# A decoder layer on one core: order and place of small operations in the head, earlier partial projections, and a new end of the expert stage

## The chip, the core and the metric

The kernel runs on one core of a Trainium2 chip. TensorE (PE) multiplies matrices, its weight loads are shown apart (PEld); VectorE (DVE), ScalarE (ACT) and GpSimd (POOL) work on tiles, SyncE (SP) starts almost all transfers. Each engine works off its own queue in order. The metric is the device time of one execution in microseconds.

## What is computed

The reference is one decoder layer on 256 tokens of 2048 columns. Cut to what matters here:

```python
mod = silu(c) @ w_ada + b_ada                   # 6 x 2048: shifts, scales, gates
sh_a, sc_a, gt_a, sh_m, sc_m, gt_m = split(mod, 6)
h = rmsnorm(x, norm_mix_g) * (1 + sc_a) + sh_a
x = x + gt_a * hybrid_mixer(h, ...)             # h @ w_in, MLA attention, mLSTM, gates, w_out
h = rmsnorm(x, norm_ffn_g) * (1 + sc_m) + sh_m
x = x + gt_m * hier_moe(h, ...)                 # router: 1 of 4 groups, 2 of its 8 experts
```

The router picks two of 32 experts for each token. The transfers of one execution move 561 MB, most of it weights.

## The kernel before

**Layout.** Activations lie transposed, 128 columns of the model on the partitions and 256 tokens along a tile, so that a row block k (of KT = 16) is 128 rows of the weights. `big` has 9 buffers of 1 MB (`u8`) for raw weights and a few large tiles, `w4` 3 of the same size (`w8`) for weights split in two, PSUM 8 banks. SyncE's queue follows the program's order (`manual_schedule`); on the other engines a scheduler orders instructions by its own estimate, except where `keep_in_program_order` pins them.

**Start.** cond = silu(c) spread over 128 partitions; the squares of x summed over partitions by 16 matmuls with a matrix of ones (ssum, L208); rstd by Ln and Exp (L157, L158).

**Head, 21 to 182 us.** A loop over k. Each row block loads three tiles on SyncE: ada tile 16 + k and ada tile k (1 MB each), and the 11 column blocks of w_in that are needed first (w_head, 704 KB). VectorE multiplies an ada tile with cond and sums along the row (L143): a column of mod. From the first comes gs = (mod + 1 + b) * gain (L151), from the second mod + b (L146). Then hp = x * gs * rstd (L805) on VectorE, h = hp + mod (L808) on ScalarE, hh = h rounded to fp32r (L811), hl = h - hh (L812). For k < WHOLE = 8 TensorE multiplies in fp32 as it is, 11 matmuls (22 passes) into six banks `hb` (L810). From k = 8 the weights are split into a rounded part and a rest (`split`, L186 on ScalarE and L187 on VectorE, tile `whl`), and three matmuls (`mm3`: L199, L200, L201) take the place of one. `push` splits a tile at once and emits its matmuls when the next has been pushed.

From k = 8 the loop also works on other columns of w_in: `first_halves` gives 14 pieces, six pairs of q/k columns of the mLSTM, v and o, each over row blocks 0 to 7 alone. `half_pair` loads 1 MB of `w_half`, runs 96 passes into a bank `hp`, and `keep_part` copies the bank to a tile `part` (L322, ScalarE). After the loop the second halves run over row blocks 8 to 15, and `add_part` adds them (L328, VectorE).

**Middle, to 780 us.** Attention, mLSTM, gates, w_out and the router; TensorE works nearly all the time.

**Experts, to the end.** Experts are ranked by their number of tokens, and stacks of four ranks (HEAVY, LIGHT) are worked off, the slabs read through a ring of buffers (`fetch_used`; a slab of an unused expert is not read). In `stack`, each of four chunks of w_down multiplies into a bank `yb`, f = 0 to 3 over the rows of four slabs; `finish` splits it into yh (L1314, ScalarE) and yl (L1315, VectorE); `combine` multiplies by the tokens' weights (L1324, L1325, banks `ob`) and `accumulate` adds to xs (L1231). A chunk is combined after the next one's matmuls, the last at the end. `store` writes 4 of 16 row blocks out.

Then follow two parts for rare cases: a last stack under `tc.If` (L1403), if its first rank has tokens, and a loop over experts with too many tokens (L1409, count read at L1408). In the execution shown both are jumped over.

## Time and profile before

| | us |
|---|---|
| median of three executions (1630.15 to 1633.23) | 1631.26 |
| the profiled execution | 1634.16 |
| its span, first to last instruction | 1632.3 |
| TensorE busy | 1360.1 (83%) |
| VectorE busy | 816.4 (50%) |
| ScalarE busy | 504.9 (31%) |
| mean granted TensorE clock | 0.933 |

The profiled execution lies 2.90 us above the median; 1.86 us of it lie outside the span. The chain of work that ended last is TensorE's by 51% and transfers' by 34%. A stage table (busy time of each engine in stretches of the span) is the best first view, since the stages have different limits: the head, the middle and the experts each look unlike the mean.

### The profile page before, as it was taken

Reading aid. Unit: us, or ns where it says so; the run is one execution under the profiler, and the core shown is the slowest. Engines: PE = TensorE matmul, PEld = TensorE weight load, DVE = VectorE, ACT = ScalarE, POOL = GpSimd, SP = SyncE. Lnnn points to the kernel's source line nnn. Section 1 sums busy time; section 2 is a strip of 40 time slices with the busy share of each in tenths; the row PEclk is TensorE's granted clock in tenths of the full one; section 3 lists DMA queues with packets and bytes.
Section 4 is the critical chain, followed back from the end, with each engine's and each line's share of the span. In section 5 each row is a group of like instructions: output and inputs, shape, how many; then the busy total and the mean of one; then the engine's idle time right before and its main releaser. Section 6 shows DMA issues by size and latency. Waiting matters only on the chain.

```text
span 1632.3 us, 24652 instructions
## 1 busy us (share of the span) xinstructions
PE 1360.1 (83%) x9726; PEld 1004.2 (62%) x9726; DVE 816.4 (50%) x1177; ACT 504.9 (31%) x720; POOL 90.5 (6%) x91
## 2 busy tenths in 40 slices
PE   7799998999999999999796696978668857567665
PEld 5598997899999989989662354645323313213212
DVE  5878699879766789986411431343111301201202
ACT  3134765446645574444311110321100101001000
POOL 0150013000000010121000000000000000000000
PEclk9999999999999999999997799999889987867998
DMA  9988767878676779874589999999999999999995
GB/s 381 369 307 328 272 230 283 317 287 303 243 273 235 276 271 413 322 292 151 228 362 382 371 392 420 374 422 396 411 420 421 420 422 421 421 421 421 421 421 223
DMA packets 78462, 560.96 MB, mean 344 GB/s; under 512 B 8705, under 2 KB 8961, under 8 KB 11905
## 3 DMA queue, kind: packets, MB, share of 16 engines
q1 hardware_dynamic: 78050, 558.84, 86.6%
q8 instruction: 80, 1.31, 0.3%
q10 hardware_dynamic: 288, 0.45, 0.1%
q14 instruction: 44, 0.36, 0.1%
HBM read 569.74 MB, written 2.10 MB: 350 GB/s over the span
## 4 chain that ended last, share of the span: by engine, by line
PE 51%; DMA 34%; DVE 9%; ACT 3%; issue 2%; POOL 0%; SPq 0%; DVEq 0%; POOLq 0%; ACTq 0%
DMA ring<-in_w_gu_dram 22%; DMA ring<-in_w_dn_dram 11%; PE gu L1285 6%; PE ga L199 4%; PE ga L201 4%; PE ga L200 4%; DVE raw L143 4%; PE yb L1285 3%; DVE whl L187 2%; PE hp L201 2%; PE hp L199 2%; PE hp L200 2%; PE xb L1259 2%; PE wo L199 1%; PE wo L201 1%
## 5 line engine op out<-in xcount | busy, mean ns | idle before, releaser
L1285 PE MATMUL gu<-ring,xg 128*32 128x512 f32 (+1 forms) x1664 | 256.5, 714 | 131.2 <-DMA ring<-in_w_gu_dram 131.0
L187 DVE TENSOR_TENSOR whl<-raw,whl 128x1024 fp32r<-128x1024 f32 (+1 forms) x222 | 267.7, 1213 | 95.5 <-ACT whl L186 95.0
L186 ACT ACTIVATE whl<-raw 128x1024 fp32r<-128x1024 f32 (+1 forms) x222 | 229.6, 1038 | 266.7 <-PE ga L201 62.7
L1285 PEld LDWEIGHTS gu<-ring,xg 128*32 128x32 f32 (+1 forms) x1664 | 63.6, 130 | 304.3 <-DMA ring<-in_w_gu_dram 157.5
L143 DVE SCALAR_TENSOR_TENSOR raw<-raw,cond 128x2048 f32<-128x2048 f32 x96 | 220.4, 2297 | 15.2 <-DMA raw<-in_w_ada_dram 15.2
L1285 PE MATMUL yb<-ring,aT 128*32 128x512 f32 (+1 forms) x832 | 130.4, 723 | 76.7 <-DMA ring<-in_w_dn_dram 75.3
L199 PE MATMUL ga<-hh,whl 128*128 128x256 f32 x512 | 149.6, 292 | 0.0
L201 PE MATMUL ga<-hh,whl 128*128 128x256 f32 x512 | 145.0, 283 | 1.4 <-DVE whl L187 1.3
L200 PE MATMUL ga<-hl,whl 128*128 128x256 f32 x512 | 144.8, 283 | 0.0
L1285 PEld LDWEIGHTS yb<-ring,aT 128*32 128x32 f32 (+1 forms) x832 | 33.7, 131 | 156.9 <-issue 115.9
L1251 DVE TENSOR_REDUCE wc<-cb 128x1 f32<-128x256 f32 x7 | 3.0, 425 | 208.7 <-PE cb L1248 208.7
L1231 DVE SCALAR_TENSOR_TENSOR xs<-ob,mod,xs 128x256 f32<-128x256 f32 x112 | 46.4, 476 | 119.0 <-PE ob L1325 119.0
L187 DVE TENSOR_TENSOR whl<-rawb,whl 128x1024 fp32r<-128x1024 f32 x36 | 43.0, 1222 | 116.5 <-ACT whl L186 116.4
L199 PEld LDWEIGHTS ga<-hh,whl 128*128 128x128 f32 x512 | 97.9, 191 | 5.1 <-issue 3.5
L201 PEld LDWEIGHTS ga<-hh,whl 128*128 128x128 f32 x512 | 97.9, 191 | 2.0 <-DVE whl L187 2.0
L200 PEld LDWEIGHTS ga<-hl,whl 128*128 128x128 f32 x512 | 98.0, 191 | 1.0 <-issue 0.7
L201 PE MATMUL hp<-hh,whl 128*128 128x256 f32 x320 | 91.0, 284 | 3.4 <-DVE whl L187 3.3
L199 PE MATMUL hp<-hh,whl 128*128 128x256 f32 x320 | 92.0, 287 | 0.0
L200 PE MATMUL hp<-hl,whl 128*128 128x256 f32 x320 | 90.5, 283 | 0.0
L1303 ACT ACTIVATE s<-gu 128x512 f32<-128x512 f32 x7 | 4.2, 597 | 273.9 <-PE gu L1285 273.9
L186 ACT ACTIVATE whl<-rawb 128x1024 fp32r<-128x1024 f32 x36 | 36.8, 1053 | 163.1 <-DMA rawb<-in_w_dn_dram 76.2
L201 PE MATMUL gu<-xgh,whl 128*128 128x258 f32 x256 | 72.1, 285 | 2.2 <-DVE whl L187 2.2
(418 smaller groups left out, 2846.0 us busy)
## 6 DMA issues: line engine op xcount, KB each, us to landing
ring<-in_w_gu_dram SPq DMA_DIRECT2D x208, 1024.0 KB, 14.6
ring<-in_w_dn_dram SPq DMA_DIRECT2D x104, 1024.0 KB, 15.5
raw<-in_w_ada_dram SPq DMA_DIRECT2D x96, 1024.0 KB, 6.9
raw<-in_w_blk_dram SPq DMA_DIRECT2D x32, 1024.0 KB, 5.1
raw<-in_w_half_dram SPq DMA_DIRECT2D x20, 1024.0 KB, 6.8
raw<-in_w_out_dram SPq DMA_DIRECT2D x16, 1024.0 KB, 6.6
raw<-in_w_head_dram SPq DMA_DIRECT2D x16, 704.0 KB, 6.6
rawb<-in_w_gu_dram SPq DMA_DIRECT2D x10, 1024.0 KB, 8.9
```

What stands on the lines that cost most here:

```text
L143: vec.scalar_tensor_tensor(raw, raw, 1.0, cond, op0=ALU.mult, op1=ALU.mult, accum_out=mod[:, i:i + 1])
L186: keep(act.activation(hi, raw, AF.Copy))
L187: keep(vec.tensor_tensor(lo, raw, hi.bitcast(F32), op=ALU.subtract))
L199: pe.matmul(out, wh, xh, start=first, stop=False)
L200: pe.matmul(out, wh, xl, start=False, stop=False)
L201: pe.matmul(out, wl, xh, start=False, stop=last)
L1231: vec.scalar_tensor_tensor(xs[:, d], src, mod[:, 80 + d:81 + d], xs[:, d], op0=ALU.mult, op1=ALU.add)
L1251: vec.tensor_reduce(wc, cb[:, :T], axis=AX.X, op=ALU.add)
L1259: pe.matmul(b[:, i * P:(i + 1) * P], xr[tt][:, k * P:(k + 1) * P], gt[tt], start=tt == 0, stop=tt == 1)
L1285: return lambda: pe.matmul(out[j * C:(j + 1) * C, :], x[:, k * P + j * C:k * P + (j + 1) * C], ws[j][:, cut], start=first, stop=stop)
L1303: act.activation(s, gu[0], AF.Silu)
```

## The change

- *Start:* the squares are added up on VectorE in part; 6 matmuls instead of 16.
- *Row blocks:* gs and mod + b are each one ScalarE operation on a column (with gbias = (1 + b) * gain worked out once). VectorE's order is pinned: product for tile 16 + k, hl of the block before, product for tile k, hp. For k >= 8 hl is a plain subtraction from an h that ScalarE writes.
- *Quarters:* the first half of each of the six q/k pairs is cut in two. Row blocks 0 to 3 of it (`quarter`, 512 KB, 24 passes after the split of half a tile) run after blocks 4 to 7 (1, 2, 1, 2 pieces); row blocks 4 to 7 stay in `first_halves`, now with `add_part` instead of `keep_part`. The weights' layout in memory is changed to match.
- *Loads:* const goes from block 0 to block 10, the router's weights from ScalarE's queue to SyncE's.
- *Experts:* in the last stack's last chunk the four slabs are read in two parts each (f = 0 to 2, then f = 3); chunk 2 is combined ahead of f = 3; `finish` works in two halves.
- *Rare cases:* the router works out one number (`spill[33]`) that is not zero if either case occurs, and one `tc.If` holds both.

```diff
@@ -136,22 +136,21 @@
     vec.tensor_scalar(bada1, col("b_ada", 0, 96), 1.0, None, op0=ALU.add)
+    gbias = keep.tile([P, KT], F32, name="gbias")
+    vec.tensor_tensor(gbias, bada1[:, KT:2 * KT], col("mix_g", 0, KT), op=ALU.mult)
@@ -200,12 +199,19 @@
         pe.matmul(out, wh, xl, start=False, stop=False)
         pe.matmul(out, wl, xh, start=False, stop=last)
 
-    ssum = bank("ssum")
+    ssum, sums = bank("ssum"), [None, None]
     for i in range(8):
-        sq = pair("sq")
-        act.activation(sq, xs[:, 2 * i:2 * i + 2], AF.Square)
+        sq = t2("sq")
+        act.activation(by2(sq), xs[:, 2 * i:2 * i + 2], AF.Square)
+        if sums[i // 6] is None:
+            sums[i // 6] = sq
+        elif i < 6:
+            vec.tensor_tensor(sums[0], sums[0], sq, op=ALU.add)
+        if i == 7:
+            sums.append(sq)
+    for i, sq in enumerate(sums):
         for j in range(2):
-            pe.matmul(ssum[:, :T], ones, sq[:, j], start=i + j == 0, stop=i + j == 8)
+            pe.matmul(ssum[:, :T], ones, sq[:, j * T:(j + 1) * T], start=i + j == 0, stop=i + j == 3)
     rstd = t2("rstd")
     rsqrt(rstd[:, :T], ssum[:, :T], D)
 
@@ -289,12 +295,22 @@
-    def half_pair(src, half, after):
-        raw = load(src[half])
+    def half_pair(src, half, after, quarters=(0, 1)):
+        q0, q1 = quarters[0], quarters[-1] + 1
+        raw = u8("raw")[:, :(q1 - q0) * 1024]
+        nc.sync.dma_start(raw, src[half][:, q0 * 1024:q1 * 1024])
         b = bank("hp")
-        for i in range(2):
-            push_block(raw[:, i * 1024:(i + 1) * 1024], b[:, i * T:(i + 1) * T], 8, lambda k: hhk(k + 8 * half),
-                       lambda k: hlk(k + 8 * half), (lambda: after(b)) if i else None)
+        for q in quarters:
+            def fn(wh, wl, q=q):
+                for i in range(2):
+                    for j in range(4):
+                        k, s = 8 * half + 4 * q + j, slice((4 * i + j) * P, (4 * i + j + 1) * P)
+                        mm3(b[:, i * T:(i + 1) * T], wh[:, s], wl[:, s], hhk(k), hlk(k), q == q0 and i + j == 0,
+                            q == q1 - 1 and i == 1 and j == 3)
+            push(raw[:, (q - q0) * 1024:(q - q0 + 1) * 1024], fn, (lambda: after(b)) if q == q1 - 1 else None)
+
+    def quarter(i):
+        half_pair(w_half[i], 0, keep_part(("qk", i)), (0,))
@@ -332,7 +348,7 @@
 
     def first_halves():
         for i in range(6):
-            half_pair(w_half[i], 0, keep_part(("qk", i)))
+            half_pair(w_half[i], 0, add_part(("qk", i)), (1,))
             yield
         for nh in range(2):
             yield from v_half(nh, 0, keep_part(("v", nh, 0), ("v", nh, 1)))
@@ -787,34 +803,47 @@
+    def lower(k, h):
+        tc.keep_in_program_order(vec.tensor_tensor(hlk(k), h, hhk(k).bitcast(F32), op=ALU.subtract))
...
+    above = None
     for k in range(KT):
-        ada(16 + k)
-        ada(k)
+        tc.keep_in_program_order(ada(16 + k))
+        if above:
+            lower(*above)
+        tc.keep_in_program_order(ada(k))
         raw = u8("raw")[:, :HEAD_N * P]
         nc.sync.dma_start(raw, w_head[k])
-        if k == 0:
+        if k == 10:
...
-        ada_gain(0, k, k + 1, 16, "mix_g")
-        ada_bias(k, k + 1)
+        act.activation(gs[:, 0, k:k + 1], mod[:, 16 + k:17 + k], AF.Identity, bias=gbias[:, k:k + 1], scale=col("mix_g", k))
+        act.activation(mod[:, k:k + 1], mod[:, k:k + 1], AF.Identity, bias=col("b_ada", k))
         hp = t2("hp")
-        vec.scalar_tensor_tensor(hp[:, :T], xs[:, k], gs[:, 0, k:k + 1], rstd[:, :T], op0=ALU.mult, op1=ALU.mult)
+        h = hp[:, T:]
+        tc.keep_in_program_order(vec.scalar_tensor_tensor(hp[:, :T], xs[:, k], gs[:, 0, k:k + 1], rstd[:, :T],
+                                                          op0=ALU.mult, op1=ALU.mult))
+        act.activation(h, hp[:, :T], AF.Identity, bias=mod[:, k:k + 1])
+        act.activation(hhk(k), h, AF.Copy)
+        above = (k, h)
...
         if k < WHOLE:
-            h = hp[:, T:]
-            act.activation(h, hp[:, :T], AF.Identity, bias=mod[:, k:k + 1])
...
-            act.activation(hhk(k), h, AF.Copy)
-            vec.tensor_tensor(hlk(k), h, hhk(k).bitcast(F32), op=ALU.subtract)
...
+            while k > 3 and n_quarter < 6 * (k - 3) // 4:
+                quarter(n_quarter)
+                n_quarter += 1
+            if k == WHOLE - 1:
+                lower(*above)
+                above = None
             continue
-        act.activation(hhk(k), hp[:, :T], AF.Identity, bias=mod[:, k:k + 1])
-        vec.scalar_tensor_tensor(hlk(k), hp[:, :T], mod[:, k:k + 1], hhk(k).bitcast(F32), op0=ALU.add, op1=ALU.subtract)
+        lower(*above)
+        above = None
@@ -1205,8 +1240,9 @@
-        spill = small("spill", [1, 33], I32)
-        vec.tensor_copy(spill, lb3[0:1, 0:33])
+        spill = small("spill", [1, 34], I32)
+        vec.tensor_copy(spill[:, 0:33], lb3[0:1, 0:33])
+        vec.tensor_tensor(spill[:, 33:34], lb3[0:1, 32:33], rest, op=ALU.add)
@@ -1309,10 +1345,12 @@
         aT = s2("aT")
         act.activation(aT, ab, AF.Copy)
 
-        def finish(ch, yb):
+        def finish(ch, yb, parts=1):
             yh, yl = s2("yh", F32R), s2("yl", F32R)
-            act.activation(yh, yb, AF.Copy)
-            vec.tensor_tensor(yl, yb, yh.bitcast(F32), op=ALU.subtract)
+            for i in range(parts):
+                s = slice(i * 512 // parts, (i + 1) * 512 // parts)
+                act.activation(yh[:, s], yb[:, s], AF.Copy)
+                vec.tensor_tensor(yl[:, s], yb[:, s], yh[:, s].bitcast(F32), op=ALU.subtract)
             return ch, yh, yl
 
         def combine(ch, yh, yl):
@@ -1328,17 +1366,28 @@
 
         done = None
         for ch in range(4):
-            ws = [fetch_used(expert_slab(n, w_dn, ch), n) for n in ranks]
+            final = last and ch == 3
+            assert not (final and room)
+            ws = [fetch_used(expert_slab(n, w_dn, ch), n, 3 * 512 if final else None) for n in ranks]
             yb = bank("yb")
             calls = [packed(yb, aT, f, ws, slice(f * 512, (f + 1) * 512), f == 0, f == 3) for f in range(4)]
             together(calls[0])
-            for group in calls[1:]:
+            for group in calls[1:3]:
                 for call in group:
+                    call()
+            if final:
+                for n, slot in zip(ranks, ws):
+                    nc.sync.dma_start(slot[:, 3 * 512:], expert_slab(n, w_dn, ch)[:, 3 * 512:], cond=used(n))
+                combine(*done)
+                done = None
+                together(calls[3])
+            else:
+                for call in calls[3]:
                     call()
             if done:
                 combine(*done)
-            done = finish(ch, yb)
-            if last and ch == 3:
+            done = finish(ch, yb, 2 if final else 1)
+            if final:
                 assert streams[0] is None
                 for i in range(3):
                     store(i)
@@ -1400,27 +1449,29 @@
-    with tc.If(nc.values_load(R["order"][0:1, 32 + LAST[1]:33 + LAST[1]], min_val=0, max_val=2 * T) != 0):
-        for _ in stream([LAST]):
-            pass
-        for k in range(4):
-            store(k)
-    n_spill = nc.values_load(R["spill"][0:1, 32:33], min_val=0, max_val=NE - 1)
-    with tc.For_i(0, n_spill, 1) as i:
...
+    ring[:] = [slot for slot in ring if not any(slot is b for b in borrowed)]
+    with tc.If(nc.values_load(R["spill"][0:1, 33:34], min_val=0, max_val=2 * T + NE) != 0):
+        with tc.If(nc.values_load(R["order"][0:1, 32 + LAST[1]:33 + LAST[1]], min_val=0, max_val=2 * T) != 0):
+            for _ in stream([LAST]):
+                pass
+            for k in range(4):
+                store(k)
+        n_spill = nc.values_load(R["spill"][0:1, 32:33], min_val=0, max_val=NE - 1)
+        with tc.For_i(0, n_spill, 1) as i:
```

How the instructions stand on the engines, at the three places that matter.

ScalarE, from row block 4 to 5, before (L808 writes h of a block, L811 rounds it):

```order
L808 ACTIVATE hp_277<-hp_277,mod_75 128x256
L811 ACTIVATE hh_149<-hp_277 128x256
L808 ACTIVATE hp_303<-hp_303,mod_75 128x256
L811 ACTIVATE hh_149<-hp_303 128x256
L808 ACTIVATE hp_329<-hp_329,mod_75 128x256
```

The same place after (L830 and L831 are h and its rounding, L824 and L825 the two column operations, L185 the split of a quarter's weights, L338 the copy of a finished quarter from bank hp_290):

```order
L830 ACTIVATE hp_273<-hp_273,mod_75 128x256
L831 ACTIVATE hh_146<-hp_273 128x256
L185 ACTIVATE whl_291<-raw_288 128x1024
L824 ACTIVATE gs_76<-mod_75,gbias_106,cols_73 128x1
L338 ACTIVATE part_350<-hp_290 128x512
L825 ACTIVATE mod_75<-mod_75,cols_73 128x1
L830 ACTIVATE hp_305<-hp_305,mod_75 128x256
L831 ACTIVATE hh_146<-hp_305 128x256
```

A split, two column operations and the copy of the quarter stand between the h of one block and the h of the next.

VectorE, from row block 8 to 9, before (L143 is the product with an ada tile, L187 the rest of a weight split, L817 hl):

```order
L805 SCALAR_TENSOR_TENSOR hp_408<-xs_72,gs_76,rstd_146 128x256
L817 SCALAR_TENSOR_TENSOR hl_152<-hp_408,mod_75,hh_150 128x256
L187 TENSOR_TENSOR whl_439<-raw_436,whl_439 128x1024
L187 TENSOR_TENSOR whl_457<-raw_436,whl_457 128x1024
L143 SCALAR_TENSOR_TENSOR raw_484,mod_75<-raw_484,cond_91 128x2048
L151 TENSOR_SCALAR gs_76<-mod_75,bada1_77,cols_73 128x1
L805 SCALAR_TENSOR_TENSOR hp_494<-xs_72,gs_76,rstd_146 128x256
L143 SCALAR_TENSOR_TENSOR raw_487,mod_75<-raw_487,cond_91 128x2048
L146 TENSOR_TENSOR mod_75<-mod_75,cols_73 128x1
L187 TENSOR_TENSOR whl_498<-raw_490,whl_498 128x768
L817 SCALAR_TENSOR_TENSOR hl_152<-hp_494,mod_75,hh_150 128x256
```

The same place after (L145 is the product, L186 the rest of a split, L808 hl, L344 the addition of a quarter from bank hp_627 to its part):

```order
L828 SCALAR_TENSOR_TENSOR hp_570<-xs_72,gs_76,rstd_143 128x256
L808 TENSOR_TENSOR hl_149<-hp_570,hh_147 128x256
L186 TENSOR_TENSOR whl_628<-raw_625,whl_628 128x1024
L145 SCALAR_TENSOR_TENSOR raw_646,mod_75<-raw_646,cond_91 128x2048
L344 TENSOR_TENSOR part_350<-hp_627,part_350 128x512
L145 SCALAR_TENSOR_TENSOR raw_649,mod_75<-raw_649,cond_91 128x2048
L828 SCALAR_TENSOR_TENSOR hp_656<-xs_72,gs_76,rstd_143 128x256
L186 TENSOR_TENSOR whl_661<-raw_652,whl_661 128x768
L186 TENSOR_TENSOR whl_689<-raw_652,whl_689 128x640
L186 TENSOR_TENSOR whl_713<-raw_710,whl_713 128x1024
L808 TENSOR_TENSOR hl_149<-hp_656,hh_147 128x256
```

The two column operations are gone, one weight split of two is gone, an addition that reads PSUM stands between the two products, and hl of block 9 stands behind three splits.

TensorE's end, before (L1285 is yb, L1324 and L1325 the combination, L1403 the If):

```order
L1324 MATMUL ob<-gT,yh 128x256
L1325 MATMUL ob<-gT,yl 128x256
L1285 MATMUL yb<-ring,aT 32x512 x16
L1324 MATMUL ob<-gT,yh 128x256
L1325 MATMUL ob<-gT,yl 128x256
```

The same place after (L1321 is yb, L1362 and L1363 the combination):

```order
L1363 MATMUL ob<-gT,yl 128x256
L1321 MATMUL yb<-ring,aT 32x512 x12
L1362 MATMUL ob<-gT,yh 128x256
L1363 MATMUL ob<-gT,yl 128x256
L1362 MATMUL ob<-gT,yh 128x256
L1363 MATMUL ob<-gT,yl 128x256
L1362 MATMUL ob<-gT,yh 128x256
L1363 MATMUL ob<-gT,yl 128x256
L1362 MATMUL ob<-gT,yh 128x256
L1363 MATMUL ob<-gT,yl 128x256
L1321 MATMUL yb<-ring,aT 32x512 x4
L1362 MATMUL ob<-gT,yh 128x256
```

The sixteen matmuls of the last chunk are parted into twelve and four, with the combination of chunk 2 between them.

## Rows read from the trace of the kernel before

**Rows 1.** Windows: us, their length, busy time (instructions), TensorE clock, DMA share, GB/s

```profile
21.00:49.75 28.75, 20.06 (x88) 16.39 (x88) 23.53 (x33) 4.30 (x11) 0.00 (x0) 1.00 0.98 399
49.75:79.33 29.58, 21.75 (x88) 17.57 (x88) 25.07 (x35) 5.20 (x11) 5.57 (x5) 0.94 0.89 353
79.33:124.40 45.07, 42.68 (x334) 41.82 (x335) 36.31 (x41) 18.21 (x23) 25.22 (x18) 0.96 0.86 315
124.40:182.50 58.10, 57.18 (x388) 52.70 (x387) 45.58 (x55) 27.11 (x35) 0.00 (x0) 1.00 0.90 343
182.50:780.00 597.50, 588.16 (x4488) 550.73 (x4487) 493.17 (x627) 334.11 (x452) 59.31 (x64) 1.00 0.74 273
780.00:1613.50 833.50, 607.94 (x4265) 312.05 (x4263) 183.55 (x371) 104.02 (x173) 0.00 (x0) 0.88 0.97 399
1613.50:1632.30 18.80, 5.99 (x42) 2.95 (x42) 3.91 (x9) 0.60 (x1) 0.00 (x0) 0.71 0.21 79
```

**Rows 2.** Timeline of one row block: start us, us, engine, line, operation, idle before

```profile
55.89 0.16 DVE L146 TENSOR_TENSOR mod<-mod,cols 128x1 f32<-128x1 f32 x1
56.08 0.51 ACT L808 ACTIVATE hp<-hp,mod 128x256 f32<-128x256 f32 x1 [5.94 <-DVE mod L146]
56.64 5.01 PE L810 MATMUL hb<-hp,raw 128*128 128x256 f32 x22 [1.88 <-ACT hp L808]
...
63.54 0.70 PE L810 MATMUL hb<-hp,raw 128*128 128x256 f32 x2 [1.88 <-ACT hp L808]
```

**Rows 3.** Timeline, an ada tile of block 4: SyncE's issue, VectorE's use

```profile
34.13 1.41 SPq L142 DMA_DIRECT2D raw<-in_w_ada_dram  x2
...
46.67 2.28 DVE L143 SCALAR_TENSOR_TENSOR raw<-raw,cond 128x2048 f32<-128x2048 f32 x1
```

**Rows 4.** Page, DMA issues: count, KB each, us from issue to landing

```profile
raw<-in_w_ada_dram SPq DMA_DIRECT2D x96, 1024.0 KB, 6.9
```

**Rows 5.** Timeline at the start, VectorE and ScalarE

```profile
16.88 0.16 DVE L146 TENSOR_TENSOR mod<-mod,cols 128x1 f32<-128x1 f32 x1
18.87 0.47 ACT L157 ACTIVATE rstd<-ssum,epsc 128x256 f32<-128x256 f32 x1 [4.16 <-PE ssum L208]
```

**Rows 6.** Groups by shape, whole run: out<-in, xcount, busy us, mean ns, idle before

```profile
L187 DVE TENSOR_TENSOR whl<-raw,whl 128x1024 fp32r<-128x1024 f32 x206 | 253.8, 1237 | 94.5 <-ACT whl L186 94.0
...
L328 DVE TENSOR_TENSOR part<-hp,part 128x512 f32<-128x512 f32 x10 | 6.8, 684 | 1.9 <-PE hp L201 1.8
...
L933 ACT ACTIVATE bias<-gu 128x1 f32<-128x1 f32 x16 | 2.6, 168 | 24.7 <-PE gu L201 24.7
```

**Rows 7.** Windows, one stretch of dense TensorE work

```profile
110.00:124.40 14.40, 14.13 (x118) 14.14 (x119) 12.18 (x15) 6.20 (x8) 0.00 (x0) 1.00 0.83 306
```

**Rows 8.** Timeline between row blocks 8 and 9

```profile
89.69 0.60 ACT L322 ACTIVATE part<-hp 128x512 f32<-128x512 f32 x1 [6.43 <-PE hp L201]
...
91.46 0.62 PE L199 MATMUL hb<-hh,whl 128*128 128x256 f32 x3 [1.81 <-ACT hh L816]
```

**Rows 9.** Windows, block 7, with a lower granted clock

```profile
70.43:79.33 8.90, 6.70 (x22) 5.27 (x22) 7.78 (x11) 2.42 (x5) 5.57 (x5) 0.81 0.62 207
```

**Rows 10.** Chain that ended last, after the last slab landed; start us, us

```profile
1613.52 3.62 PE yb L1285 x26
...
1619.51 0.61 DVE yl L1315
...
1622.01 0.47 DVE xs L1231
```

**Rows 11.** Queue instructions of two lines, duration ns min/median/max, start us

```profile
L1403 PEldq TENSOR_LOAD <-order x1: 1024/1024/1024, 1620.2 to 1620.2; - x1
...
L1403 PEldq COMPARE_BRANCH  x1: 3810/3810/3810, 1621.3 to 1621.3; - x1
...
L1409 PEldq COMPARE_BRANCH  x3: 85/203/4132, 1625.9 to 1631.2; - x3
```

**Rows 12.** Stores of the output tile, from issue to landing

```profile
DMA to landing us min/median/max: 2.7/3.3/3.9
```

56 lines of the change are left out of this document (30 added, 26 removed).

## The prediction

> **What bounds the kernel now.** I read the table by stage first [rows 1]: each stage has another limit. From 21 to 79 us, row blocks 0 to 7, DMA share is .98 and .89, VectorE 23.53 of 28.75 us and 25.07 of 29.58, TensorE only 20 to 22 us. From 79.33 to 182.50 TensorE is busy 42.68 of 45.07 and 57.18 of 58.10 us: it is the limit, VectorE and DMA stand at .78 to .90. From 182.50 to 780 TensorE is busy 588 of 597.5 us. From 780 to 1613.50 the DMA share is .97: expert slabs. The last 18.80 us are a chain with 5.99 us of TensorE in them. The change touches the first 180 us and the tail; the order between them is almost the same on each engine, so what the head gains or loses passes to the end one for one, since no stage behind it waits for anything else than its predecessor.
>
> In blocks 0 to 7 the block's timeline [rows 2] shows a loop of 6.89 us (56.64 to 63.54 for the first matmuls of two blocks): VectorE works off one ada tile, the small addition, then ScalarE makes h, then 22 passes of TensorE in 5.01 us. That loop is VectorE's: an ada tile issued at 34.13 is worked on only at 46.67 [rows 3], though a transfer of its kind lands in 6.9 us [rows 4].
>
> **The change part by part.** All against the profiled execution, 1634.16 us, which is 2.90 above the median 1631.26.
>
> *Start-up.* Ten of sixteen sum-of-squares matmuls go, five additions on VectorE come. No gain: rstd's Ln now stands on ScalarE behind the addition for block 0, which needs the second ada tile; before, that was done at 16.88 + .16 and Ln ran at 18.87 [rows 5]. Five additions of some .68 us (128x512, priced by a later row of that shape [rows 6]) delay the two tiles' 4.6 us to about 17.4, table load and Ln follow, and h(0) comes at 22.2 as now. 0, bounds -1 to +1.
>
> *Blocks 0 to 3.* A fixed order moves the subtraction, and both small operations (.16 the one [rows 2]) leave VectorE: its two products, hp and the subtraction are about 5.4 us of the 6.89. The loads don't get faster: 1 + 1 + .69 MB in 6.89 us are 410 GB/s, and DMA share is .98 already. But a tile no longer lies in its buffer for 4.5 us: block 4's second one, issued by 35.2, lands at 42.1; 2.3 for the product and 1.0 for addition, hp and h, and block 4 starts at about 45.4 instead of 49.75. It is a backlog worked off once, not a shorter period. **-4.3.**
>
> *Blocks 4 to 7, six quarters.* One quarter is 24 passes of .12 us (14.13 us for 118 [rows 7]), 2.9 us; six are 17.3 us, moved from blocks 8 to 15 to here. TensorE then needs 4 x 5.01 + 17.3 = 37.4 us where the stage took 29.58. But there is a hold: by the order ScalarE copies a quarter out of PSUM (.60) ahead of the addition (.17) and h (.51) of the next block, so the next block's matmuls can't start until the last quarter has left TensorE and those three are done. Before, such a pattern in one place cost 1.81 us of idle TensorE behind the part's copy at 89.69, up to 91.46 [rows 8]. Four times 1.7 makes 6.8: 44.2 us, **+14.6** (bounds +7.8 without holds, +14.6).
>
> *Blocks 8 to 15.* 17.3 us of TensorE work are gone; what of it is time? Busy was 99.9 of 103.2 us, so at most 17.3 comes back, if nothing else binds: VectorE's 81.9 us lose the six split halves (6 x 1.24 [rows 6]) and the small operations, some 71 remain; DMA at .88 of 103 us loses 3 MB, some 83 remain; TensorE 82.6. Three engines at 71 to 83 us, in a fixed order: additions of a part (.68) stand on VectorE between the two ada tiles of the next block and wait there for TensorE's hp, and behind them queue hp, hl and the weight splits for which TensorE waits. A walk through the eight blocks with the row durations, every hold taken in full, gives 99.7 us for the seven intervals where 101 were, that is only 1.3 back. The row of before speaks against the walk: with copies in the same in-order place all idle of these stages is 2.39 + .92 us. Between 1.3 and 17.3 I take **-8**, a little nearer the walk, since the additions' place is new and no row shows it.
>
> *Head:* -4.3 + 14.6 - 8 = **+2.3**; bounds by the ends above +9 (walk) and, with neither hold, -4.3 + 7.8 - 17.3 = -13.8, of which I count -8 as reachable (DMA and VectorE are near TensorE's sum).
>
> The change puts an addition of one column on ScalarE, and here a rule speaks against it. Row: an ACTIVATE of 128x1 took 168 ns [rows 6], VectorE's addition .16 us [rows 2]. The Trainium skill, ScalarE: Activation LUTs (Rules for kernel authors), sends add and mul to VectorE, and its section What ACT_TABLE_LOAD costs gives an ACTIVATE 186 ns + .833 per element and 93 more for each column operand, so some .28 and .37 here. The row agrees roughly with the base figure and shows no case with two column operands; by the page the four held blocks would be .1 to .2 us longer each, .6 in all.
>
> *Clock.* Granted clock was .81 in block 7 [rows 9], where the 22 passes took 6.70 instead of 5.01: such a fall is 1.7 us. More idle in TensorE may add one, a denser 45 to 80 us may remove one: 0, bounds +-1.7.
>
> *Router.* Two tiny operations: +.2.
>
> *Tail.* Chain before [rows 10], L = landing of the last slab, 1613.5, where yb starts: 26 records of yb 3.62, ob, then VectorE finishes the four accumulations of chunk 2 (to 1619.51) before it can do yl of chunk 3, then ob and four accumulations, store issued at 1622.5 = L + 9.0. After: chunk 2 is combined ahead of f = 3, and the four first parts, three quarters of the bytes of the four slabs, have come 2.6 us before L (1 MB at the stage's 399 GB/s). yb of f = 0 to 2 is done at about L, ob to L + 1.1, the 8 records of f = 3 (.139 each) to L + 2.2; half yh and half yl .7, ob .7, four accumulations 1.7: store issued at about L + 5.5. **-3.5.**
> Behind it TensorE's queue jumps over two bodies: 3810 ns for the If and, after another load, 4132 ns for the loop [rows 11]. One branch remains: TensorE's ob ends at about L + 4.2, its register load 1.0 [rows 11], one jump 3.8 to 4.1, last barrier about 1: end at L + 11 to 12.6, and the store's landing (2.7 to 3.9 us [rows 12]) with SyncE's waits fits under that. Before: L + 18.8. So -6.2 to -7.8; eight loads instead of four may put L .3 to 1 later. **-6.5**, bounds -8.5 and -4.
>
> *Sum:* 1634.16 + 2.3 + .2 - 6.5 = 1630.2; less the 2.90 above the median: **1627.3 us**.
>
> **The rivals.**
> *A, the forecast:* half the moved work comes back. 1624 to 1631.
> *B, no holds.* ScalarE's copies and VectorE's additions find TensorE done early enough, and the moved quarters fill idle TensorE as their place suggests (8 us idle of each 28 in blocks 0 to 7). Head -8 to -3: 1617 to 1622. For it: 2.39 us idle in the stage that has such copies already. Against: the order puts each copy directly ahead of the next block's h.
> *C, slower.* The walk in full: additions on VectorE wait for TensorE and TensorE for what is behind them; head +9, and one more clock fall of 1.7; with the tail at -4 to -6.5 that is 1634 to 1638. It decides from a head loss of 9.6 us on (tail 6.5 + .2% of 3.26 less .2). For it: one start per block depends on ScalarE, VectorE and TensorE in turn. Against: the walk adds all holds.
> *D, the tail doesn't do what it says:* the one branch costs as much as two (the jump's time depends on what lies behind it, which no row separates), only 3 us come: 1629.5 to 1632, same.
>
> **How the numbers follow.** A .43, B .27, C .20, D .10. 0.2%, 3.26 us, is about what a measurement can tell from no change: faster is under 1628.0. A gives .26 faster, .17 same; B .27 faster; C .15 slower and .05 same (its mildest form, without the clock fall, is 1634.0); D .01 faster, .09 same. Faster .54, same .31, slower .15. The range from 1618 to 1635.5 leaves out the lower end of B and the upper of C, about .2.
>
> **What would show it.** First hb of block 4 at about 45.4 and of block 8 near 89.5 (B: 83), with gaps of 1.3 to 1.8 us whose releaser is ScalarE's h behind a copy. Blocks 8 to 15 over at 184.8; idle of TensorE there about 9 us, released by VectorE's hl or ScalarE's hh (C: 17; B: under 5). The store near L + 5.5, one long branch on TensorE's queue, end at L + 12.3. Wrong would be: hb(8) before 84, or an end of the tail after L + 15.

## The result, and the profile after

| | median us | ratio to the kernel before, 95% interval |
|---|---|---|
| kernel before, beside it | 1632.24 | |
| changed kernel | 1643.30 | 1.0063, 1.0042 to 1.0084 |

The change makes the kernel slower, by some 10 us; 1627.3 and faster were forecast. The profiled execution of the changed kernel took 1636.99 us, the shortest of its four (1636.99 to 1644.1), and that of before 1634.16, among the longest; the two traces side by side thus show less than the medians, and I compare them stage by stage.

The table by stage of the changed kernel, which answers to [rows 1] (length, busy time of TensorE, weight loads, VectorE, ScalarE, GpSimd, granted clock, DMA share, GB/s):

```profile
21.00:49.75 28.75, 23.43 (x80) 19.32 (x81) 21.13 (x25) 7.44 (x18) 0.00 (x0) 0.77 0.79 318
49.75:79.33 29.58, 27.09 (x163) 24.72 (x162) 19.37 (x21) 10.08 (x19) 0.00 (x0) 1.00 0.97 378
79.33:124.40 45.07, 32.77 (x229) 30.71 (x228) 31.11 (x36) 17.59 (x30) 24.09 (x22) 0.92 0.72 262
124.40:182.50 58.10, 51.84 (x313) 46.10 (x312) 43.86 (x48) 24.76 (x39) 0.00 (x0) 0.94 0.86 319
```

TensorE is busier where the quarters came (27.09 us where it was 21.75) and, in the same two stretches where it had been busy for 42.68 and 57.18 us, it now idles for 12.3 and 6.3. The stretches are the same in time, so the changed kernel, which is behind by then, is at earlier row blocks in them. No engine and no transfer is near its limit between 79 and 124 us: .72 of the DMA time, 31 of 45 us of VectorE. And three of the four stretches have a lower clock than before: .77, .92 and .94, where it was 1.00, .96 and 1.00.

Events of both traces, in us (before, changed kernel): first matmul of row block 0 at 22.2, 23.2; h of block 4 ready near 49.7, 50.5, and its first matmul at 49.8, 51.7; first matmul of block 8 at 79.3, 94.8, of block 15 at 181.6, 195.5; the head's result first used at 182.6, 197.2; first expert slab requested at 779.7, 796.0; last slab of chunk 2 there at 1606.1, 1614.9; end of the span at 1632.3, 1634.8. So the head is 14.6 us longer. From there to the first slab it is 597.1 and 598.8 us. From the first slab to chunk 2's last it is 826.4 and 818.8: that stage took 819 to 829 us in the profiled runs that work on the same numbers, with the same slabs in the same order, and is no part of the change. From chunk 2's last slab to the end it is 26.2 and 19.9.

Row blocks 8 to 15 by themselves, from the first matmul of block 8 to the first use of the head's result, before and in the changed kernel (same columns):

```profile
79.33:182.59 103.26, 99.95 (x720) 94.61 (x721) 81.89 (x95) 45.32 (x59) 25.22 (x18) 0.98 0.88 330
```

```profile
94.84:197.19 102.35, 87.25 (x580) 80.29 (x581) 74.72 (x81) 43.22 (x69) 19.44 (x18) 0.93 0.81 296
```

TensorE has 140 recorded passes less and is busy 12.7 us less, but the time is only .9 us shorter: its idle time grew from 3.3 to 15.1 us.

The end of the changed kernel, chain of work that ended last (start us, us, what), answering to [rows 10], and the queue instructions behind it, answering to [rows 11]:

```profile
1614.89 3.62 PE yb L1321 x26
...
1619.66 3.53 PE yb L1321 x23
...
1624.33 1.12 PE yb L1321 x8
...
1626.76 0.42 DVE yl L1353
1627.18 1.21 DVE xs L1267 x3
```

```profile
L1453 PEldq TENSOR_LOAD <-spill x1: 502/502/502, 1627.2 to 1627.2; - x1
...
L1453 PEldq COMPARE_BRANCH  x1: 3507/3507/3507, 1627.8 to 1627.8; - x1
```

There is one long branch, 3507 ns, where there were two, and behind the last matmuls stand two half passes of yh and yl. The last slabs no longer end the chain: TensorE works through chunk 2, the first parts and the second parts without waiting for a transfer.

Now the head. The first stretch in fine windows (same columns as above), and three events:

```profile
22.20:25.00 2.80, 1.77 (x4) 1.50 (x5) 2.80 (x4) 1.05 (x3) 0.00 (x0) 0.58 1.01 421
25.00:28.00 3.00, 3.00 (x8) 2.37 (x8) 3.00 (x5) 0.68 (x3) 0.00 (x0) 0.50 0.40 164
28.00:31.00 3.00, 3.00 (x12) 2.46 (x11) 3.00 (x4) 1.20 (x3) 0.00 (x0) 0.76 0.00 0
31.00:34.00 3.00, 3.00 (x16) 2.64 (x15) 1.95 (x3) 1.22 (x3) 0.00 (x0) 1.00 0.51 160
```

```profile
31.33 0.33 SPq L817 DMA_DIRECT2D raw<-in_w_head_dram  x1
...
37.98 2.29 DVE L145 SCALAR_TENSOR_TENSOR raw<-raw,cond 128x2048 f32<-128x2048 f32 x1 [5.03 <-DMA raw<-in_w_ada_dram]
...
43.88 12.73 PE L835 MATMUL hb<-hp,raw 128*128 128x256 f32 x44 [3.08 <-ACT hp L830]
```

The granted clock is .50, the lower of the two levels (1.2 GHz), from 25 to 28 us, after TensorE had stood still twice (9.6 to 13.9 and 19.4 to 23.2 us: the ten matmuls that went had filled the first gap). Block 0's matmuls end late, its weight tile is given back late, SyncE's queue stands at block 2's weight tile until 31.33, and from 25 to 34 us the transfers move 40, 0 and 51% of what they can. Before, that tile was requested at 27.24. Block 3's ada tiles stand behind it in the queue, and VectorE then waits 5.03 us for one of them.

That the new start makes this fall is not shown. The version with one branch alone (below) has the start of before, without the first gap, and its trace has it too:

```profile
23.00:36.00 13.00, 12.76 (x44) 10.32 (x44) 11.36 (x15) 1.29 (x3) 0.00 (x0) 0.76 0.67 261
```

Of ten traces here with the start of before, five have a clock below 1.00 from 23 to 36 us; of nine without it, all nine.

Between blocks 4 and 8 (start, us, engine, line; idle before and who ended it):

```profile
59.51 0.60 ACT L338 ACTIVATE part<-hp 128x512 f32<-128x512 f32 x1 [3.11 <-PE hp L200]
...
60.88 5.01 PE L835 MATMUL hb<-hp,raw 128*128 128x256 f32 x22 [1.41 <-ACT hp L830]
...
72.73 5.02 PE L835 MATMUL hb<-hp,raw 128*128 128x256 f32 x22 [1.08 <-ACT hp L830]
...
82.02 5.02 PE L835 MATMUL hb<-hp,raw 128*128 128x256 f32 x22 [1.41 <-ACT hp L830]
...
94.84 0.50 PE L198 MATMUL hb<-hh,whl 128*128 128x256 f32 x2 [2.06 <-ACT hh L831]
```

These are the holds that the prediction priced: the copy, the addition, h, and TensorE idle for 1.1 to 2.1 us at each of four blocks, 6.0 in all where 6.8 were forecast. From the first matmul of block 4 to that of block 8 it is 43.1 us; 44.2 were forecast.

Behind block 8, one period:

```profile
102.19 0.69 DVE L344 TENSOR_TENSOR part<-hp,part 128x512 f32<-128x512 f32 x1 [2.79 <-PE hp L200]
102.80 2.28 DVE L145 SCALAR_TENSOR_TENSOR raw<-raw,cond 128x2048 f32<-128x2048 f32 x1
...
105.01 0.61 DVE L828 SCALAR_TENSOR_TENSOR hp<-xs,gs,rstd 128x256 f32<-128x256 f32 x1
...
105.12 0.29 ACT L825 ACTIVATE mod<-mod,cols 128x1 f32<-128x1 f32 x1 [4.46 <-DVE raw L145]
...
105.54 3.22 DVE L186 TENSOR_TENSOR whl<-raw,whl 128x768 fp32r<-128x768 f32 x3
...
106.35 1.04 ACT L185 ACTIVATE whl<-raw 128x1024 fp32r<-128x1024 f32 x1
...
107.44 0.58 PE L198 MATMUL hp<-hh,whl 128*128 128x256 f32 x1 [5.29 <-ACT whl L185]
108.68 0.94 DVE L808 TENSOR_TENSOR hl<-hp,hh 128x256 fp32r<-128x256 f32 x1
```

VectorE's addition waits 2.79 us for TensorE's last matmul of a quarter. Only then come the second product, hp, three splits and hl, 6.8 us in a row; ScalarE's addition waits 4.46 us for that product, with a split of weights behind it that TensorE stands still for, 5.29 us. TensorE waits for VectorE, and VectorE for TensorE.

### The profile page after: what moved, and what is told of

Its sections match the earlier page's. It is cut to its first block, busy times and chain, and to the rows that moved or that the text cites. A ratio compares the mean times of both kernels' runs of the same rounds, so it can differ in the third digit from the quotient of the medians.

```text
span 1634.8 us, 24639 instructions
## 1 busy us (share of the span) xinstructions
PE 1364.2 (83%) x9706; PEld 1008.3 (62%) x9706; DVE 814.9 (50%) x1160; ACT 515.1 (32%) x759; POOL 80.4 (5%) x91
## 4 chain that ended last, share of the span: by engine, by line
PE 47%; DMA 34%; DVE 10%; ACT 4%; issue 3%; SPq 1%; POOL 1%; DVEq 0%; ACTq 0%; POOLq 0%
DMA ring<-in_w_gu_dram 22%; DMA ring<-in_w_dn_dram 9%; PE gu L1321 6%; DVE whl L186 3%; PE yb L1321 3%; DVE raw L145 3%; PE ga L198 3%; PE ga L200 3%; PE ga L199 3%; PE hb L835 2%; PE hp L200 2%; PE xb L1295 2%; PE hp L198 2%; PE hp L199 2%; PE wo L198 1%
## 5 line engine op out<-in xcount | busy, mean ns | idle before, releaser
L1321 PE MATMUL gu<-ring,xg 128*32 128x512 f32 (+1 forms) x1664 | 257.9, 718 | 128.3 <-DMA ring<-in_w_gu_dram 128.2
L186 DVE TENSOR_TENSOR whl<-raw,whl 128x1024 fp32r<-128x1024 f32 (+1 forms) x222 | 266.0, 1206 | 106.8 <-ACT whl L185 106.2
L185 ACT ACTIVATE whl<-raw 128x1024 fp32r<-128x1024 f32 (+1 forms) x222 | 228.9, 1037 | 262.3 <-PE ga L200 64.6
L1321 PEld LDWEIGHTS gu<-ring,xg 128*32 128x32 f32 (+1 forms) x1664 | 64.7, 130 | 301.6 <-DMA ring<-in_w_gu_dram 154.0
L145 DVE SCALAR_TENSOR_TENSOR raw<-raw,cond 128x2048 f32<-128x2048 f32 x96 | 220.6, 2303 | 20.0 <-DMA raw<-in_w_ada_dram 18.5
L1321 PE MATMUL yb<-ring,aT 128*32 128x512 f32 (+1 forms) x832 | 128.9, 716 | 70.8 <-DMA ring<-in_w_dn_dram 69.3
L1321 PEld LDWEIGHTS yb<-ring,aT 128*32 128x32 f32 (+1 forms) x832 | 33.2, 130 | 149.2 <-issue 113.1
L186 DVE TENSOR_TENSOR whl<-rawb,whl 128x1024 fp32r<-128x1024 f32 x36 | 43.0, 1222 | 107.9 <-ACT whl L185 106.1
L185 ACT ACTIVATE whl<-rawb 128x1024 fp32r<-128x1024 f32 x36 | 36.8, 1054 | 158.3 <-DMA rawb<-in_w_gu_dram 70.5
```

What stands on the lines that cost most here:

```text
L145: return vec.scalar_tensor_tensor(raw, raw, 1.0, cond, op0=ALU.mult, op1=ALU.mult, accum_out=mod[:, i:i + 1])
L185: keep(act.activation(hi, raw, AF.Copy))
L186: keep(vec.tensor_tensor(lo, raw, hi.bitcast(F32), op=ALU.subtract))
L1321: return lambda: pe.matmul(out[j * C:(j + 1) * C, :], x[:, k * P + j * C:k * P + (j + 1) * C], ws[j][:, cut], start=first, stop=stop)
```

## The experiments

Ratios are to the kernel before, timed on the same chip. "Old start" is the start of before: 16 matmuls for the sum of squares, and block 0's column operations on VectorE.

**The new end alone**, on the kernel before.

```diff
+            final = last and ch == 3
-            ws = [fetch_used(expert_slab(n, w_dn, ch), n) for n in ranks]
+            ws = [fetch_used(expert_slab(n, w_dn, ch), n, 3 * 512 if final else None) for n in ranks]
...
+    with tc.If(nc.values_load(R["spill"][0:1, 33:34], min_val=0, max_val=2 * T + NE) != 0):
```

> The kernel before with the new end alone: last chunk's slabs in two parts, chunk 2 combined ahead, two-half finish, one branch for both rare cases; head and row blocks as before. If the whole loss of the changed kernel lies in the head, this is faster than before by the tail's 6.5 us (1625.7). Rival, the tail's gain is only one of its two halves: 1628 to 1629. Rival, the end of the changed kernel is itself late, because TensorE has to redo its order there: 1632 or more.

1627.29 us, .9972 (.9957 to .9986): 4.6 us (2.3 to 7.0) faster. Its trace has 20.0 us from chunk 2's last slab to the end, where before had 26.2. The tail does what it says, and the head owes the rest: by the ratios 1.0063 / .9972, that is .91% or 15 us, close to the traces' 14.6.

**One branch alone**, on the kernel before.

> The kernel before with the one branch for both rare cases alone; slabs whole, finish whole. If both halves of the new end are worth what the trace of before says, the branch gives 3 us of the 6: 1628. Rival, the branch gives nothing, since another engine or the store ends as late: 1631.

1628.58 us, .9984 (.9971 to .9996), 2.6 us. In its trace the last slab lands at 1608.6 and the span ends at 1624.0, 15.4 us later, where before took 18.8. Both halves of the end are real, some 3 us each in the traces.

**The sum of squares as before**, in the changed kernel.

```diff
-    ssum, sums = bank("ssum"), [None, None]
+    ssum = bank("ssum")
...
+            pe.matmul(ssum[:, :T], ones, sq[:, j], start=i + j == 0, stop=i + j == 8)
```

> The changed kernel with the sum of squares as before (16 matmuls, no additions on VectorE). Start-up theory: TensorE's idle 9.6 to 13.9 us before the sum makes the granted clock .50 for blocks 0 and 1, the first weight tile is given back 4 us late, the transfers stand for 6 us; without it block 4 starts 4 to 5 us earlier and the end comes 4 to 5 us earlier, about 1638.5. Rival, the holds in blocks 4 to 15 set the pace anyway: the 4 us are swallowed there, 1642 to 1643.

1640.40 us, 1.0068 (1.0041 to 1.0094): nothing won. Block 0 still began at 22.9: the sum's matmuls took 9.8 us (9.2 before), rstd waited for the last of them until 19.5 us (18.9 before), and the clock was .78 from 23 to 36 us. The gap ahead of the sum was gone, from 9.7 us on TensorE had work, and the fall was still there; so a second run took the whole start back:

```diff
+        if k == 0:
+            vec.tensor_scalar(gs[:, 0, k:k + 1], mod[:, 16 + k:17 + k], bada1[:, 16 + k:17 + k], col("mix_g", k), op0=ALU.add, op1=ALU.mult)
+            ada_bias(k, k + 1)
...
```

> The changed kernel with the whole start of before: 16 matmuls for the sum, both column operations of block 0 on VectorE, rstd ahead of block 1's column operations on ScalarE. The run with the old sum alone began block 0 at 22.9 and still had a granted clock of .78 from 23 to 36. Start theory: block 0 at 22.2 with the clock at 1.00, the first weight tile given back by 27.5 and DMA share over .9 from 23 to 36; 4 us earlier at the end, about 1638.5. Rival, later holds swallow it: 1642 to 1643.

1640.63 us, 1.0059 (1.0039 to 1.0080). The stretch from 23 to 36 us:

```profile
23.00:36.00 13.00, 12.66 (x58) 10.53 (x57) 11.06 (x13) 3.21 (x9) 0.00 (x0) 1.00 0.80 319
```

Clock 1.00 and DMA share .80 (.52 in the changed kernel): the fall is gone, and block 8 begins at 91.4 instead of 94.8. But the head's end is at 198.2, no earlier: blocks 8 to 15 swallow the 3.4 us. This is the trace of the slowest of its five executions, and the median lies between the two forecasts; by the ratios (1.0059 and 1.0063) nothing clear of the intervals is won, as the rival has it.

**Without the early quarters**, in the changed kernel.

```diff
-            half_pair(w_half[i], 0, add_part(("qk", i)), (1,))
+            half_pair(w_half[i], 0, keep_part(("qk", i)))
...
-            while k > 3 and n_quarter < 6 * (k - 3) // 4:
+            while False:
```

> The changed kernel without the early quarters: the six column pairs run over row blocks 0 to 7 in one piece as before, from block 8 on; pinned order and ScalarE's column operations stay. Hold theory (copies and additions of quarters make TensorE wait): 10 to 11 us come back, about 1632.5; block 8 starts near 84. Rival, the pinned order of VectorE is what holds: 1640 or more.

1631.47 us, 1.0004 (.9993 to 1.0015). Some 10 us come back, block 8 begins at 79.7. The quarters are the larger part of the loss.

**VectorE's order free**, quarters in place: `keep_in_program_order` taken off the four operations of a row block.

> The changed kernel with VectorE's row-block order left to the scheduler; quarters stay. Hold theory: within 3 us of 1643. Rival, the pinned order costs the time: 1633 or less.

1635.92 us, 1.0025 (1.0011 to 1.0039), about 6 us better than pinned: neither theory's number. The pinned order is a part of the loss, with the quarters: in the trace blocks 8 to 15 take 99.4 us instead of 102.4.

**Each without the other.** Quarters alone, on before's order, and the order alone, without quarters; both with the new end and the old start.

> The kernel before with the new end and the early quarters alone; VectorE's order, the column operations and the start as before. Theory that the quarters are the loss by themselves: 8 to 10 us above the new end alone (1627.3), 1635 to 1637. Rival, they cost only together with the pinned order: under 1631.

> The kernel before with the new end, the pinned order and ScalarE's column operations, with the start of before and no quarters. The run without quarters lost the 4 us of the new end to its start (clock .87 and DMA share .62 from 23 to 36). Start theory: those come back, 1626 to 1628. Rival, the pinned order costs them elsewhere: 1630 or more.

1630.66 us, .9990 (.9974 to 1.0006), and 1628.87 us, .9981 (.9967 to .9996). Against the new end alone (.9972) the quarters cost 3 us and the order 1.5, neither clear of the intervals; together, with the old start (1.0059), they cost 14. That is 10 us more than the sum of the two, 4 to 15 by the intervals. Under the first pair of theories the rival came out: quarters lose much only with the pinned order. Of the second pair, the median lies between the two, and the start theory is not borne out: the trace of the order alone has a clock of .78 and a DMA share of .56 from 23 to 36 us, below the .87 and .62 of the run without quarters. The heads of single traces show less of this: they end at 184.9 us with the new end alone, 191.7 with the quarters, 188.3 with the order and 198.2 with both.

Where the two meet is shown by blocks 8 to 15 alone, from block 8's first matmul to the head's end, in us, one trace each:

| VectorE's order | column pairs whole, from block 8 on | first quarters moved ahead |
|---|---|---|
| left to the scheduler | 103.3 (before), 105.6 (new end alone), 103.9 (one branch alone) | 98.6 (quarters alone), 99.4 (order free), 94.7 (order free, old start) |
| pinned | 107.5 (without quarters), 107.9 (order alone) | 102.4 (changed), 104.3 (old sum), 106.8 (old start) |

With the order free the stretch gets some 7 us shorter, by the means, when the quarters leave it; with the order pinned some 3, and it is longer in either column. The same head differs by up to 2.3 us between traces (first field).

**Which part of the order**: the column operations back on VectorE with the order pinned; and the order free with the column operations on ScalarE; both with quarters and old start. The edit of the first, against the run with the whole start of before:

```diff
-        if k == 0:
+        if True:
             vec.tensor_scalar(gs[:, 0, k:k + 1], mod[:, 16 + k:17 + k], bada1[:, 16 + k:17 + k], col("mix_g", k), op0=ALU.add, op1=ALU.mult)
```

> The changed kernel with the old start and both column operations on VectorE in every block; quarters, pinned order and new end stay. Its twin with the operations on ScalarE was 1.0059 of before. Theory that ScalarE's addition, which waits for the second ada product, stands ahead of the weight splits that TensorE waits for: the head falls back to that of the quarters alone, .999 to 1.001 (1630 to 1634). Rival, the pinned order of VectorE by itself (product behind an addition that waits for TensorE): 1.004 or more.

> The changed kernel with the old start and VectorE's row-block order left to the scheduler; quarters and the column operations on ScalarE stay. Theory that ScalarE's addition is the hold, whatever VectorE's order: 1.003 to 1.006. Rival, only the pinned order holds: .999 to 1.001, as for the quarters alone.

1649.32 us, 1.0103 (1.0081 to 1.0126), and 1635.09 us, 1.0027 (1.0013 to 1.0041). My theory that ScalarE's addition is the hold falls: with it gone the pinned kernel is worse. With the order free the second figure is what the first theory asked for, so ScalarE's operations may cost some 6 us there, against the quarters alone; between these two kernels the form of hl and two loads differ as well, and the heads of their traces end at 190.9 and 191.7 us, so that is not shown.

The second run and the one with the whole old start differ in the four pins alone: 1.0027 against 1.0059, and in blocks 8 to 15, pinned and then free:

```profile
91.42:198.20 106.78, 91.44 (x580) 84.64 (x581) 74.81 (x81) 43.19 (x69) 19.86 (x18) 0.89 0.78 286
```

```profile
96.20:190.89 94.69, 83.68 (x575) 77.28 (x576) 75.59 (x81) 42.47 (x67) 24.33 (x18) 0.96 0.88 320
```

With nearly the same number of passes, splits and products, the pinned order takes 12 us longer in these traces, the first of which is of the slowest of its five executions; by the ratios it is 5 us.

**Additions and copies moved.** The additions behind hp of the next block, pinned; the copies behind the next block's h, pinned (with h and its rounding pinned on ScalarE in every block); and both with the old start. Of the edits, the one for the additions:

```diff
+    def flush_late():
+        for key, b in late:
+            tc.keep_in_program_order(vec.tensor_tensor(part[key], b, part[key], op=ALU.add))
+        late.clear()
```

> The changed kernel with each addition of a quarter put behind hp of the next row block on VectorE (pinned there), so that no product with an ada tile stands behind it. Theory that VectorE's additions hold buffers, loads and weights in blocks 8 to 15: DMA share from 90 to 135 rises from .72 to over .8, 5 to 8 us come back, 1635 to 1638. Rival, the copies in blocks 4 to 7 and the start make the loss: 1642 to 1643.

> The changed kernel with each copy of a quarter in blocks 4 to 7 put behind h of the next row block on ScalarE (pinned). Theory that the copies hold TensorE between blocks 4 and 8: 1 to 1.4 us of idle less at four places, 4 to 5 us earlier, about 1639. Rival, the transfers set the pace there (DMA share .97): TensorE waits as long for something else, 1642 to 1643.

> The three edits together: old start, late additions, late copies; quarters, pinned order and new end stay. If start, additions and copies are the whole loss, their 12 to 15 us come back: 1628 to 1631. If the quarters gain once nothing holds them, less than the new end alone (1627.3). Rival, the transfers of the head (its DMA share is already .83 to .98 before) leave no room, and the 3 MB moved forward cost something by themselves: 1633 or more.

1646.64 us, 1.0101 (1.0076 to 1.0127); 1646.25 us, 1.0098 (1.0072 to 1.0123); 1649.76 us, 1.0118 (1.0090 to 1.0146). All three lose, where all three should have won. They lose it in blocks 8 to 15 (111.5, 109.5 and 114.2 us instead of 102.4), and each has pinned more operations. The trace of the first shows what came next:

```profile
108.04 1.06 ACT L185 ACTIVATE whl<-raw 128x1024 fp32r<-128x1024 f32 x1 [5.58 <-PE hb L200]
...
109.13 1.23 DVE L186 TENSOR_TENSOR whl<-raw,whl 128x1024 fp32r<-128x1024 f32 x1 [4.75 <-ACT whl L185]
110.27 2.83 DVE L145 SCALAR_TENSOR_TENSOR raw<-raw,cond 128x2048 f32<-128x2048 f32 x1
...
117.47 1.23 PE L198 MATMUL hb<-hh,whl 128*128 128x256 f32 x4 [4.88 <-ACT hh L841]
```

ScalarE waits 5.58 us for TensorE to give back a buffer of split weights (there are three), VectorE's rest of that split waits 4.75 us for ScalarE, both products stand behind it, and TensorE waits 4.88 us for the h that follows from them. So the hold was not the place of these instructions; with one moved, the next in the circle holds.

**Buffers and loads.** Two quarter tiles in one buffer; and the later quarters without loads. The edit of the second:

```diff
-        raw = u8("raw")[:, :(q1 - q0) * 1024]
-        nc.sync.dma_start(raw, src[half][:, q0 * 1024:q1 * 1024])
+        if quarters == (1,):
+            raw = cond[:, 1024:]
...
```

> The changed kernel with two quarter tiles (512 KB each) in one 1 MB buffer of the pool, instead of one buffer for each half-filled tile; nothing else changed. Buffer theory: from block 8 four buffers are left for raw weights, loads wait in SyncE's queue for a free one, and a half-filled buffer halves what is under way; with packing DMA share from 95 to 125 rises from .65 to .8 and 4 to 8 us come back, 1633 to 1637. Rival, buffers are not what binds: 1640 to 1643.

> The changed kernel whose six later quarters take their weights from a tile that is there anyway (cond), so the six column pairs come out of other weights in row blocks 4 to 7: no load, no buffer, 3 MB less, and the same instructions on all engines. If loads and buffers hold blocks 8 to 12: 8 us or more come back, under 1634. Rival, the order of copies, additions and splits on ScalarE and VectorE holds them whatever the loads do: 1639 or more.

1644.71 us, 1.0085 (1.0063 to 1.0108), nothing won by packing. Without the loads the time itself (1606.83 us) can't be compared, since other numbers reach the router and other slabs are read; the head can. Its stretch from 110 to 125 us, and the same of the changed kernel:

```profile
110.00:125.00 15.00, 11.73 (x79) 11.32 (x79) 10.50 (x12) 5.19 (x8) 2.42 (x3) 0.84 0.35 133
```

```profile
110.00:125.00 15.00, 11.73 (x89) 11.32 (x89) 9.51 (x12) 5.20 (x8) 5.12 (x6) 0.95 0.66 229
```

DMA share .35 instead of .66, and TensorE is no busier. (The equal 11.73 us are chance, 79 passes at a clock of .84 and 89 at .95.) From block 8 to the head's end it is 102.1 us, where it was 102.4. The loads of the quarters and their buffers don't hold these blocks.

**The chain itself.** Left over was the theory that a row block's own chain (product, mod, h, splits, with three buffers between) has about the period that TensorE's work had, and was covered by it: the work took as long as the chain, so the chain's waits cost nothing.

> The changed kernel without the first ada tile (16 + k) in row blocks 8 to 15: no load, no product, its column is copied from one eight blocks earlier, so the gains of these blocks are other numbers; what is read is the head alone (first hb of block 8 to the first use of its end, 102.4 us in the changed kernel). Cover theory: with the quarters gone TensorE's work no longer covers the block's chain of loads, products and splits, so the chain sets the pace, and eight blocks without 2.3 us of product and 1 MB are 12 us or more shorter, under 90. Rival, something else on TensorE or ScalarE sets it: over 98.

> The kernel before with the same piece left out (first ada tile of blocks 8 to 15; other numbers, only the head is read: 103.3 us from block 8's first hb to the head's end). Cover theory: TensorE's 99.9 us of work set the pace there and cover the chain, so almost nothing is won: 99 or more. Rival, the chain of loads and products set the pace before as well: under 95.

The first use of the head's result, in the changed and then in the kernel before, each without the product:

```profile
L198 PE MATMUL hb<-hh,whl x88: 278/283/415, 94.8 to 189.1; 128*128 128x256 f32 x88
...
L286 ACT ACTIVATE cq<-hb x2: 589/593/597, 187.2 to 187.7; 128x512 f32<-128x512 f32 x2
```

```profile
L199 PE MATMUL hb<-hh,whl x88: 278/283/387, 79.1 to 180.6; 128*128 128x256 f32 x88
...
L280 ACT ACTIVATE cq<-hb x2: 590/596/603, 178.6 to 179.1; 128x512 f32<-128x512 f32 x2
```

From block 8's first matmul to the head's end: 92.4 us instead of 102.4 in the changed kernel, 99.5 instead of 103.3 before. The same piece is worth 10.0 us in the one and 3.8 in the other. That is what the cover theory asks for in direction and nearly in size (under 90 was expected, 99 or more for the other). The scheduler placed the additions otherwise once the product was gone, so a part of the 10 may be that; and the same head took 103.3 to 105.6 us in the three traces of the table above, so that the 3.8 may be up to 6.1. Each of the two was run once.

The runs without quarters put the cover back, with the order pinned: TensorE is then busy for 103.0 and 103.4 us instead of 87.3 to 91.4, and the stretch is only 1 to 6 us longer. That is the cover theory from the other side: most of the work that was moved away had cost no time there.

## Why the prediction was wrong

The stages below go by the first matmul of a row block, in the two profiled executions.

- *Start-up, 0 (-1 to +1).* Measured +1.0 for block 0, at the bound. What it didn't see is the clock: TensorE's second gap before block 0 grew from 3.4 to 3.9 us and a gap of 4.3 us came ahead of it, and block 0 ran at half the clock. The one branch alone has neither (3.4 us and no gap ahead) and fell as well, so the gaps are not shown to be the cause.
- *Blocks 0 to 3, -4.3.* Wrong: +.9. The backlog of 4.5 us was there, but the step followed the ada tile alone on SyncE's queue; ahead of block 3's ada tiles stands block 2's weight tile, which waits for the buffer that TensorE frees with block 0's last matmul. With block 0 late and slow, the transfers stood still instead.
- *Blocks 4 to 7, +14.6.* Right: +13.6, 43.1 us from block 4 to 8 against 44.2, and the idle times are at the four places named, behind the copies, 6.0 us against 6.8.
- *Blocks 8 to 15, -8.* This is the step that failed most. 102.4 us instead of 103.3: -.9, where the walk with every hold had -1.3 and I took -8; TensorE idled for 15.1 us, where about 9 were forecast. The walk's 99.7 us for the seven intervals are 100.7 in the trace (before has 102.2, not the 101 of the prediction). The argument against the walk was that the rows of before show 2.39 and .92 us of idle TensorE with copies in the same place [rows 1, 8]. Those holds were short because TensorE had a long stretch of work queued ahead of each, and that work is what the change moved away. Idle time under cover was read as the absence of a hold. And -8 is about what the stretch gave with VectorE's order free (94.7 to 99.4 us, 4 to 9 less than before); the pinned order, which the walk followed, took the rest.
- *Head, +2.3 (-8 to +9).* +14.6, 12.3 more than forecast: 1.0 from the start, 5.2 from blocks 0 to 3, -1.0 from blocks 4 to 7, 7.1 from blocks 8 to 15.
- *Router, +.2.* 1.7 us more from the head to the first slab in these two traces, 1.1 more with the new end alone; but the one branch alone, which has the new number in the router too, has .1 less. The stretch differs by more than that between the traces (596.9 to 600.7 us), so no cost of the new number is shown.
- *Tail, -6.5 (-8.5 to -4).* 6.3 us in the traces, 4.6 (2.3 to 7.0) by the medians; the mechanism is as told, one branch of 3.5 us and chunk 2 combined ahead. Only the place of the limit differs: the last slabs are there before TensorE gets to them.
- *First slab to chunk 2's last slab, 0.* 7.6 us quicker in the profiled run, no part of the change: that this trace is only 2.5 us longer than that of before is luck.
- *Rivals.* C was the case that came: additions wait for TensorE and TensorE for what is behind them, head loss over 9.6. It had .20, and its time (1634 to 1638) was still 5 us short: like every rival it counted on the 4.3 us of blocks 0 to 3, which didn't come. B had .27 and was a full 20 us off.
- *The clock, 0 (+-1.7).* Four falls in the head instead of two: the granted clock was .50 in 23 to 29, 43.5 to 49.5, 105 to 111 and 136 to 142 us, where before had 72 to 75 and 92.5 to 95.5. The fall at the start goes with a block 8 that begins 3.4 us later than in the run with the old start; the head ends no later.

The cause is settled as far as this: by the medians quarters and pinned order lose little each and 14 us together; the pinned order lengthens blocks 8 to 15 by some 7 us once the quarters have left them, and by some 3 while they are there; no single instruction, load or buffer of those tried is the hold. That the block's chain took the pace when its cover went is supported by the last pair of runs and by the runs without quarters, which restore it. Which wait in the pinned chain makes it longer than the free one stays open, and so does what makes the clock fall at the start.

Of the versions tried, the kernel before with the new end alone has the lowest ratio, .9972, faster than both; its interval overlaps with those of the one branch alone (.9984) and of the order alone (.9981).

## What to carry to other kernels

Idle time that is small beside a long queue of work says nothing of what the wait costs once that work is moved: price the chain that lies under the cover by its own durations, as if nothing else were there, and take that as the new period. Where a walk by row durations and an argument from small idle times disagree, the walk is the one that knows the order. An order that is pinned to help one stage is pinned in the next as well: price it there too. Moving work to where an engine idles is only a gain if the place it leaves is then limited by something shorter.

## What the runs showed of the hardware

ScalarE's operation on one column took 292 ns with one column operand and 385 with two (16 each), where the row of before that stood for them had 168 [rows 6]:

```profile
L824 ACT ACTIVATE gs<-mod,gbias,cols 128x1 f32<-128x1 f32 x16 | 6.2, 385 | 43.7 <-DVE raw L145 43.7
L825 ACT ACTIVATE mod<-mod,cols 128x1 f32<-128x1 f32 x16 | 4.7, 292 | 16.7 <-DVE raw L145 16.6
```

The figures that the Trainium skill gives (ScalarE: Activation LUTs, What ACT_TABLE_LOAD costs), .28 and .37, agree with this trace, and the nearest row did not. Its advice to add on VectorE (Rules for kernel authors) is not borne out here where VectorE's order is pinned: 1.0103 with the column operations there, 1.0059 with them on ScalarE. With the order free it is not contradicted: .9990 with them on VectorE, 1.0027 on ScalarE, in kernels that differ in more than that.
